# Neighbourhood attention layer on one core: output weights summed in memory by transfers, another order of the last products, bias tables laid out in memory, and a rearranged first step

## The chip, the cores and the metric

The kernel runs on one core of a Trainium2 chip. A core has TensorE (matrix products, PE in the profile; its weight loads are PEld), VectorE (DVE), ScalarE (ACT), GpSimd (POOL) and SyncE (SP), each with its own queue of instructions that it works through in order, and 16 DMA engines that serve transfers issued by SP, ACT and POOL. The metric is the device time of one execution in microseconds, the median of several runs. Less is better.

## The reference

One layer on 512 tokens (a grid of 8 rows by 64 columns), width 2048, 16 heads of 128, all float32:

```python
h = rms_norm(x, norm_pre)
q, k, v, z = split(h @ w_in, 4)            # w_in: 2048 x 8192
o = neighbourhood_attention(q, k, v, rpb)   # 8 x 16 window of tokens, bias rpb by relative place
y = (o * silu(z)) @ w_out                   # w_out: 2048 x 2048
out = x + rms_norm(y, norm_post)
```

The window covers all 8 rows and 16 columns, clipped at the edges of the grid. `rpb` holds 15 x 31 values for each head.

## The kernel before, in words

**Products.** Each product is taken from float32 operands split into two parts: `hi` (rounded, by a ScalarE copy, L241) and `lo` (the rest, by a VectorE subtraction, L242), and three of the four part products are summed: hi by hi, lo by hi, hi by lo. The left operand is the activations (tiles `a`, kept split in SBUF), the right one a 128 x 512 tile of weights that streams from memory.

**Steps.** Steps 0 to 7 compute the projection for two heads each. Step 8 and the last step, `LAST` = 9, compute the output product, the left and the right part of it. Steps 0 and 8 (`PLAIN`) are plain products of two halves, 32 slots of 12 matmuls. The other steps use a fast scheme on 2 x 2 blocks with seven products instead of eight: seven passes of 8 slots, 6 matmuls a slot. The passes have numbers 0 to 6 and accumulate in three chains X, Y, Z of two PSUM tiles each: passes 0 and 2 in X, 1, 3 and 5 in Y, 4 and 6 in Z. In the last step they run in the order `LATE`; before, that is 0, 1, 3, 4, 5, 6, 2.

**Weights of the seven passes.** Pass 0 uses block B11 in the tiles `T[0..7]`. Passes 1, 3 and 4 add B12, B22 and B21 to T in turn (L234, VectorE; the added block is a `raw` tile that a transfer has just brought); pass 4 then loads B12 into T; pass 5 uses B22 as it comes and adds it to T (L249), which pass 6 uses; pass 2 uses B21 as it comes. `raw` has four buffers.

**Order.** The slots are numbered through, m = 0 to 511. `prep(m)` splits the weights of slot m two slots ahead, and issues the loads of raws up to six slots ahead; the split weights have three buffers. `at(m, f)` puts f behind the matmuls of slot m: the attention of the heads of the pair before, all of whose work is spread over the slots of the next step (`HEAD`, `when`); the squares of x for the first norm (`square_x`, `begin`); evictions. A scheduler orders each engine's instructions by a plan of its own, except those issued through `sync`, `dve`, `act`, which keep the order of the program.

**The first step.** x, transposed, comes in 16 tiles (`load_x`), three slots ahead; each is scaled by the gain (L159) and split. Eight squares, each of 128 x 1024 of x in 0.5 MB, are loaded from slot 6 on and give the row sums; `rstd` turns them into `rc` at slot 28 (a power on POOL). The step's first half `U[0]` waits in PSUM and is evicted with the scale rc in slots 28 to 31 (`take_first`, L288), the second half in slot 31. Tiles of the pool `c` (six buffers of 128 x 1024) hold squares, evicted results and some x.

**Bias.** For each head one transfer on POOL brings overlapping rows of rpb (`braw`, L444), and three VectorE additions (L450) turn them with a mask into the table `bm` that the scores are added to. The gates are kept in memory and fetched again by transfers on POOL (L549, L559).

**The end.** Each of the four column quarters of the output needs a square sum over its rows (`finish`: a ScalarE square, a VectorE product with the gain); when the last quarter of a group of 128 rows is in, the row's factor `rcy` is computed (VectorE L666, POOL L667), and `final` adds the four quarters to the residual tiles `xres`, loaded before (`load_res`), and stores them. There are four such groups of rows: 2 and 3 are complete after pass 6, 0 and 1 after the two halves of the last pass, 2. The last pass does one half of its rows after the other, and so its eight weight tiles are all split beforehand, into tiles of `a` that are free by then.

Of the kernel before, what the change touches and what calls it, by code (L numbers as in the profile page):

```python
# [66 lines left out]
@with_exitstack  # L67
def na_block(ctx: ExitStack, tc: tile.TileContext, xT, x, gpre, gpost, w, rpb, mask, out):
    nc = tc.nc
    sync, dve, act = (InOrder(tc, e) for e in (nc.sync, nc.vector, nc.scalar))  # L70
    PSUM = bass.MemoryType.PSUM
# [155 lines left out]
    def prep(m):  # L227
        step, p, k = where(m)
        plain = step in PLAIN
        if step == 0 and p == 0:  # L230
            take_x(k)
        src = raws.pop(m) if is_raw(m) else T[k]
        if not plain and p in (1, 3, 4):
            nc.vector.tensor_tensor(T[k], T[k], src, ALU.add)  # L234
# [6 lines left out]
        nc.scalar.copy(hi, src)  # L241
# [41 lines left out]
    def take_first(n, j):  # L283
        c = C.setdefault(0, {})
        name = ("11", "12", "21", "22")[n + j // 2 * 2]
        if j % 2 == 0:
# [1 line left out]
        nc.scalar.activation(c[name][:, j % 2, :], U[n][j], AF.Copy, scale=rc[:, j : j + 1])  # L288

# [41 lines left out]
    def combine(step, p):  # L331
# [10 lines left out]
        elif p == 2:  # L342
            c["11"] = pair(f"c11_{step}")
            for s in range(2):
                nc.scalar.activation(c["11"][:, s, :], u[s], AF.Copy, scale=rc[:, s : s + 1])
        elif p == 3:
            c["22"] = pair(f"e_{step}")
            for s in range(2):
                nc.vector.tensor_tensor(c["22"][:, s, :], u[s], c["12"][:, s, :], ALU.subtract)
            nc.vector.tensor_tensor(c["21"], c["22"], c["21"], ALU.subtract)  # L350
        elif p == 4:
            for s in range(2):
                nc.vector.tensor_tensor(c["22"][:, s, :], u[s], c["22"][:, s, :], ALU.add)
        elif p == 5:
            for s in range(2):
                nc.vector.tensor_tensor(c["12"][:, s, :], u[s], c["12"][:, s, :], ALU.subtract)  # L356
            for s in range(2):
# [4 lines left out]
        elif step == LAST:
            c["11"] = pair(f"c11_{step}")
            for s in range(2):
                dve.tensor_tensor(c["21"][:, s, :], u[s], c["21"][:, s, :], ALU.subtract)
                dve.tensor_tensor(c["22"][:, s, :], c["22"][:, s, :], u[s], ALU.subtract)
                finish(2, 2 + s, c["21"][:, s, :])
                finish(3, 2 + s, c["22"][:, s, :])
# [72 lines left out]
    def load_bias(h):  # L441
        raw = sp.tile([P, L], F32, tag="braw", name=f"braw{h}")
        src = bass.AP(rpb.tensor, rpb.offset + h * 15 * TBL, [[1, 16], [TBL, 8], [1, 7 * TBL + 32]])
        nc.gpsimd.dma_start(raw[:, 0 : 7 * TBL + 32], src)  # L444
        bm_of[h] = (raw, sp.tile([P, 3, 256], F32, tag="bm", name=f"bm{h}"))

    def bias(h, i):
        raw, bm = bm_of[h]
        rev = bass.AP(raw.tensor, raw.offset + 7 * TBL + 31, [raw.ap[0], [-1, 32], [-TBL, 8]])
        nc.vector.tensor_tensor(  # L450
            bm[:, i, :].rearrange("p (a b) -> p a b", b=8),
            rev,
            mask_sb[:, i, :].unsqueeze(2).to_broadcast([P, 32, 8]),
            ALU.add,
        )

# [15 lines left out]
    def add_bias(h, a):  # L472
# [3 lines left out]
        for i in ((0, 1), (3, 2))[a]:  # L476
# [6 lines left out]
                in1=bm_of[h][1][:, (0, 1, 1, 2)[i], lo:hi],
# [169 lines left out]
    def finish(n, t, src, dst=None):  # L653
# [6 lines left out]
        nc.scalar.activation(rest, src, AF.Square, accum_out=part[:, t, i : i + 1])  # L660
        (dve if n > 1 else nc.vector).tensor_tensor(y, src, gb[n], ALU.mult)
        if i == 2:
            nc.vector.reduce_sum(ms3[:, col], part[:, t, 0:3], axis=mybir.AxisListType.X)
            nc.vector.tensor_scalar(ms3[:, col], ms3[:, col], 1.0 / D, EPS, ALU.mult, ALU.add)
        if i == 3:
            dve.tensor_scalar(msy[:, col], part[:, t, 3:4], 1.0 / D, ms3[:, col], ALU.mult, ALU.add)  # L666
            nc.gpsimd.tensor_tensor(rcy[:, col], msy[:, col], mhalf[:, 0:1], ALU.pow)  # L667
# [59 lines left out]

# [38 lines left out]
```

## Time and profile before

| | |
|---|---|
| median of 3 runs | 902.35 us (899.84 to 902.76) |
| profiled execution: its own time, its span | 903.68 us, 901.9 us |
| mean granted TensorE clock | 0.994 |
| busy share of the span | PE 98%, PEld 81%, DVE 84%, ACT 62%, POOL 3% |
| transfers | 163.32 MB, mean 181 GB/s |

How to read it: the span runs from the first to the last instruction. A busy share is an average over the whole span. Matmuls are pipelined, so that a busy PE can still be late; what a stretch lost is seen from the start times of its matmuls, compared with a stretch of the same work that nothing disturbs. In a row of the timeline the columns are start and length in us, engine, line, operation, output and inputs, and count; a bracket gives the idle time ahead of it and what ended it.

### The profile page before, as it was taken

The page shows a single profiled execution, that of the slowest core. Times are in us where ns is not written, and L with a number is a line of the kernel's source. Part 1 is how long each engine was busy: PE and PEld are TensorE (multiplying, and loading weights), DVE is VectorE, ACT ScalarE, POOL GpSimd, SP SyncE. Part 2 cuts the span into 40 slices and gives each one's busy share as a digit, 9 for nine tenths or more (in the row PEclk, how much of TensorE's full clock was granted, in tenths as well). Part 3 has the DMA queues.
Part 4 walks back from the last instruction along what each step waited for, and adds up shares of the span by engine and source line. Part 5 has one row for each costly group of instructions (what it writes and reads, how often), then busy time and mean ns, then how long its engine had stood idle before and what let it go on. Part 6 is the DMA issues. An engine that isn't in the chain of part 4 may idle for free. (4 is left out here: it accounts for less than half of the span.)

```text
span 901.9 us, 13169 instructions
## 1 busy us (share of the span) xinstructions
PE 880.9 (98%) x4184; PEld 731.3 (81%) x4184; DVE 755.3 (84%) x1415; ACT 561.2 (62%) x1089; POOL 29.7 (3%) x59
## 2 busy tenths in 40 slices
PE   9999999999999999999999999999999999999994
PEld 7878888888888888888888888888888788887773
DVE  5467879997989798989888987998799855887987
ACT  7566766575758575856585667566766755554461
POOL 1000000000000000000000000000010100000001
PEclk9999999999999999999999999999999999999998
DMA  8895357745773776377647764765587534549765
GB/s 256 237 258 131 105 138 210 217 130 162 219 214 111 190 227 192 95 218 210 176 112 219 210 176 110 239 200 149 137 278 205 157 93 119 158 122 254 245 179 186
DMA packets 85878, 163.32 MB, mean 181 GB/s; under 512 B 10017, under 2 KB 10017, under 8 KB 85809
## 3 DMA queue, kind: packets, MB, share of 16 engines
q1 hardware_dynamic: 82080, 151.56, 57.7%
q0 software_dynamic: 3296, 10.41, 4.2%
q8 instruction: 32, 0.52, 0.2%
q10 hardware_dynamic: 432, 0.53, 0.2%
q14 instruction: 38, 0.30, 0.1%
HBM read 154.59 MB, written 7.86 MB: 180 GB/s over the span
## 5 line engine op out<-in xcount | busy, mean ns | idle before, releaser
L241 ACT CAST hi<-t 128x512 fp32r<-128x512 f32 x320 | 196.8, 618 | 137.3 <-DVE lo L242 31.1
L242 DVE TENSOR_TENSOR lo<-t,hi 128x512 fp32r<-128x512 f32 x320 | 218.1, 687 | 25.8 <-ACT hi L241 24.9
L242 DVE TENSOR_TENSOR lo<-raw,hi 128x512 fp32r<-128x512 f32 x184 | 125.8, 689 | 62.8 <-ACT hi L241 50.3
L241 ACT CAST hi<-raw 128x512 fp32r<-128x512 f32 x184 | 113.6, 620 | 98.9 <-PE u L279 18.7
L234 DVE TENSOR_TENSOR t<-t,raw 128x512 f32<-128x512 f32 x192 | 128.5, 688 | 13.0 <-DMA raw<-in_w 12.5
L279 PE MATMUL u<-hi,a 128*128 128x512 f32 x512 | 133.1, 397 | 3.4 <-ACT hi L241 2.1
L279 PEld LDWEIGHTS u<-hi,a 128*128 128x128 f32 x512 | 96.2, 191 | 24.3 <-ACT hi L241 2.6
L279 PE MATMUL u<-lo,a 128*128 128x512 f32 x256 | 70.8, 390 | 0.0
L279 PEld LDWEIGHTS u<-lo,a 128*128 128x128 f32 x256 | 48.2, 188 | 10.1
L249 DVE TENSOR_TENSOR t<-t,raw 128x512 f32<-128x512 f32 x64 | 42.8, 688 | 1.2 <-DMA raw<-in_w 1.1
L149 DVE TENSOR_TENSOR a<-x,a 128x256 fp32r<-128x256 f32 (+1 forms) x24 | 11.6, 512 | 19.5 <-ACT a L148 19.5
L450 DVE TENSOR_TENSOR bm<-braw,mask_sb 128x256 f32<-128x256 f32 x48 | 27.4, 601 | 0.0
L322 PE MATMUL u1Y<-hi,a 128*128 128x512 f32 x96 | 26.8, 396 | 0.0
L322 PE MATMUL u6Y<-hi,a 128*128 128x512 f32 x96 | 26.8, 396 | 0.0
L322 PE MATMUL u5Y<-hi,a 128*128 128x512 f32 x96 | 26.8, 396 | 0.0
L322 PE MATMUL u7Y<-hi,a 128*128 128x512 f32 x96 | 26.8, 396 | 0.0
L322 PE MATMUL u3Y<-hi,a 128*128 128x512 f32 x96 | 26.8, 396 | 0.0
L322 PE MATMUL u4Y<-hi,a 128*128 128x512 f32 x96 | 26.8, 396 | 0.0
L322 PE MATMUL u2Y<-hi,a 128*128 128x512 f32 x96 | 26.8, 396 | 0.0
L322 PE MATMUL u9Y<-hi,a 128*128 128x512 f32 x96 | 26.6, 392 | 0.0
L444 POOL DMA_DIRECT2D braw<-in_rpb x16 | 8.5, 534 | 437.9 <-DVE bm L450 253.5
L322 PEld LDWEIGHTS u9Y<-hi,a 128*128 128x128 f32 x96 | 17.9, 188 | 4.3 <-ACT s L341 0.4
(444 smaller groups left out, 1953.2 us busy)
## 6 DMA issues: line engine op xcount, KB each, us to landing
raw<-in_w SPq DMA_DIRECT2D x384, 256.0 KB, 3.0
t<-in_w SPq DMA_DIRECT2D x128, 256.0 KB, 3.0
x<-in_xT SPq DMA_DIRECT2D x16, 256.0 KB, 4.4
xres<-in_x SPq DMA_DIRECT2D x16, 256.0 KB, 6.2
graw<-zm POOLq DMA_DIRECT2D x14, 256.0 KB, 3.7
out<-xres SPq DMA_DIRECT2D x14, 256.0 KB, 3.2
sq<-in_x SPq DMA_DIRECT2D x6, 512.0 KB, 9.4
braw<-in_rpb POOLq DMA_DIRECT2D x16, 184.0 KB, 3.6
```

Source lines behind the costliest of these rows:

```text
L149: (vector or nc.vector).tensor_tensor(lo, src, hi.bitcast(F32), ALU.subtract)
L234: nc.vector.tensor_tensor(T[k], T[k], src, ALU.add)
L241: nc.scalar.copy(hi, src)
L242: nc.vector.tensor_tensor(lo, src, hi.bitcast(F32), ALU.subtract)
L249: nc.vector.tensor_tensor(T[k], T[k], src, ALU.add)
L279: nc.tensor.matmul(U[n][j], l, r, start=k == 0 and i == 0, stop=k == KT - 1 and i == 2)
L322: nc.tensor.matmul(U[c][s], l, r, start=p in (0, 1, 4) and k == 0 and n == 0, stop=k == KH - 1 and n == 2, skip_group_check=True,)
L444: nc.gpsimd.dma_start(raw[:, 0 : 7 * TBL + 32], src)
L450: nc.vector.tensor_tensor(bm[:, i, :].rearrange("p (a b) -> p a b", b=8), rev, mask_sb[:, i, :].unsqueeze(2).to_broadcast([P, 32, 8]), ALU ...
```

## The change

- **Sums of W.** A new tile in memory, `wsum`, is filled with the four sums of blocks that the last step's passes 1, 3, 4 and 6 use: B11+B12, that +B22, that +B21, and B12+B22. For each of 8 tiles a sum is a copy from memory to memory and an accumulating transfer, 64 transfers in all, on POOL. They are issued from slot 32 on, 6 slots apart (later where the slot is in pass 2 or 5), each behind a one-column copy on ScalarE from a tile T in use and a one-column copy of that on POOL. The last step then loads each pass's tiles into T, a pass ahead, and makes no additions; only pass 2 still uses raws, which are loaded up to 24 slots ahead.
- **Order.** `LATE` becomes 0, 1, 3, 4, 6, 5, 2. The last pass's weights are split every second slot from the middle of the fifth pass on.
- **The end.** `finish` and `final` of row groups 2 and 3 are placed in the slots of the sixth pass (pass 5), and VectorE's instructions there no longer keep the program's order. Residual tiles are loaded at other slots, those of group 0 into T.
- **Bias.** The whole table of each head (128 x 3 x 256) is an input; a transfer on SP loads it. The three additions, the mask and the transfer on POOL go.
- **Gates** are stored and fetched on SP.
- **First step.** Squares are loaded from slot 10 on and squared 5 slots later; `rstd` is at slot 30. `U[0]` is evicted by plain copies in slots 17 to 20 and scaled in place in slot 31. x is fetched four slots ahead. The loads of T for step 1 keep the program's order.

The diff, cut:

```diff
-LATE = (0, 1, 3, 4, 5, 6, 2)
+LATE = (0, 1, 3, 4, 6, 5, 2)
...
     def load_t(step, q, k):
-        nc.sync.dma_start(T[k], w[step, q, k])
+        (sync if step == 1 and q == B11 else nc.sync).dma_start(T[k], w[step, q, k])
+    wsum = dp.tile([4, KH, P, L], F32, name="wsum")
+    LATE_W = {0: w[LAST, B11], 1: wsum[0], 3: wsum[1], 4: wsum[2], 5: w[LAST, B22], 6: wsum[3], 2: w[LAST, B21]}
+    SUMS = ((0, w[LAST, B11], B12), (1, wsum[0], B22), (2, wsum[1], B21), (3, w[LAST, B12], B22))
+    turns = cp.tile([P, 2, 64], F32, name="turns")
+    def sum_w(j, t):
+        i, add, k = j // 16, j // 8 % 2, j % 8
+        nc.scalar.copy(turns[:, 0, j : j + 1], t[:, 0:1])
+        pool.tensor_copy(turns[:, 1, j : j + 1], turns[:, 0, j : j + 1])
+        o, src, q = SUMS[i]
+        if add:
+            pool.dma_start(wsum[o, k], w[LAST, q, k], accum_op=ALU.add, max_dma_last_dim=8192)
+        else:
+            pool.dma_start(wsum[o, k], src[k], max_dma_last_dim=8192)
...
-        return step in PLAIN or p not in (0, 6)
+        return step in PLAIN or (p == 2 if step == LAST else p not in (0, 6))
...
-        e = max(m - 6 if m < N - KH else 0, seq[i - NRAW] if i >= NRAW else 0)
+        e = max(m - (6 if m < N - KH else 24), seq[i - NRAW] if i >= NRAW else 0)
...
-        if not plain and p in (1, 3, 4):
+        if step < NSTEP and not plain and p in (1, 3, 4):
             nc.vector.tensor_tensor(T[k], T[k], src, ALU.add)
...
-        if plain:
+        if step == LAST:
+            i = LATE.index(p)
+            if i + 2 < NPASS:
+                nc.sync.dma_start(T[k], LATE_W[LATE[i + 1]][k])
+        elif plain:
...
-        nc.scalar.activation(c[name][:, j % 2, :], U[n][j], AF.Copy, scale=rc[:, j : j + 1])
+        if n == 0:
+            nc.scalar.copy(c[name][:, j % 2, :], U[n][j])
+        else:
+            nc.scalar.activation(c[name][:, j % 2, :], U[n][j], AF.Copy, scale=rc[:, j : j + 1])
...
     def load_bias(h):
-        raw = sp.tile([P, L], F32, tag="braw", name=f"braw{h}")
...
-        nc.gpsimd.dma_start(raw[:, 0 : 7 * TBL + 32], src)
...
+        bm_of[h] = sp.tile([P, 3, 256], F32, tag="bm", name=f"bm{h}")
+        nc.sync.dma_start(bm_of[h], rpb[h])
...
-            nc.gpsimd.dma_start(graw[h], z_of[h])
+            nc.sync.dma_start(graw[h], z_of[h])
...
-        nc.gpsimd.dma_start(X[h], graw[h])
+        nc.sync.dma_start(X[h], graw[h])
...
-        for i in range(3):
-            at(when(h, i) if late else when(h, 0) - 7 + i, bias, h, i)
...
-        at(6 + 2 * i, begin, i)
-        at(12 + 2 * i, lambda i=i: pending.pop(i)())
-    at(8, lambda: nc.gpsimd.dma_start(mask_sb, mask))
-    at(28, rstd)
+        at(10 + 2 * i, begin, i)
+        at(15 + 2 * i, lambda i=i: pending.pop(i)())
+    at(30, rstd)
     for j in range(4):
-        at(28 + j, take_first, 0, j)
+        at(KT + 1 + j, take_first, 0, j)
+        at(FIRST - 1, lambda j=j: scale_c(C[0][("11", "21")[j // 2]], j % 2, j // 2 * 2))
...
-    for k in range(KH):
-        t, q = divmod(k, 4)
-        at(base(LAST) + KH + k, load_res, 2 + t, q)
-        at(base(LAST) + (5 * KH + 2 * q + 1 if t == 0 else 2 * KH + 2 * q), load_res, t, q)
+    for i, (t, q) in enumerate((t, q) for t in (2, 3, 1) for q in range(4)):
+        at(base(LAST) + (KH + 7 * i // 2 if i < KH else 4 * KH + 4 + 2 * q), load_res, t, q)
+    for q in range(4):
+        at(base(LAST) + 5 * KH + q, load_res, 0, q)
+    for j in range(64):
+        m = base(1) + 6 * j
+        while where(m)[1] in (2, 5):
+            m += 1
+        at(m, sum_w, j, T[where(m)[2]])
     for s in range(2):
-        at(base(LAST) + 6 * KH + 1 + s, final, 2 + s)
+        for n, key in ((2, "21"), (3, "22")):
+            at(base(LAST) + 5 * KH + 1 + 2 * s, lambda n=n, key=key, s=s: finish(n, 2 + s, C[LAST][key][:, s, :]))
+        for q in range(4):
+            at(base(LAST) + 5 * KH + 5 + 2 * s + q // 2, final, 2 + s, (q,))
...
-        if N - 2 * KH <= m + AHEAD < N - KH:
-            prep(m + AHEAD + KH)
-        if 0 <= m and m + 3 < KT:
-            load_x(m + 3)
+        if m >= N - 3 * KH + 4 and m % 2 == 0 and m < N - KH + 4:
+            prep(N - KH + (m - (N - 3 * KH + 4)) // 2)
+        if 0 <= m and m + 4 < KT:
+            load_x(m + 4)
```

In `combine`, `finish` and `final`, `dve.` becomes `nc.vector.`.

More of the change, by code (lines that the diff above doesn't have):

```diff
@@ L67, in na_block @@
 @with_exitstack
-def na_block(ctx: ExitStack, tc: tile.TileContext, xT, x, gpre, gpost, w, rpb, mask, out):
+def na_block(ctx: ExitStack, tc: tile.TileContext, xT, x, gpre, gpost, w, rpb, out):
     nc = tc.nc
-    sync, dve, act = (InOrder(tc, e) for e in (nc.sync, nc.vector, nc.scalar))
+    sync, dve, act, pool = (InOrder(tc, e) for e in (nc.sync, nc.vector, nc.scalar, nc.gpsimd))
     PSUM = bass.MemoryType.PSUM
@@ L99, in na_block @@
     nc.gpsimd.memset(mhalf, -0.5)
-    mask_sb = cp.tile([P, 3, 32], F32, name="mask_sb")
     edge = {}
@@ L364, in combine @@
             for s in range(2):
[L365 to L368, printed above, removed]
+                nc.vector.tensor_tensor(c["21"][:, s, :], u[s], c["21"][:, s, :], ALU.subtract)
+                nc.vector.tensor_tensor(c["22"][:, s, :], c["22"][:, s, :], u[s], ALU.subtract)
         else:
@@ L441, in load_bias @@
     def load_bias(h):
-        raw = sp.tile([P, L], F32, tag="braw", name=f"braw{h}")
[L443 to L455, printed above, removed]
+        bm_of[h] = sp.tile([P, 3, 256], F32, tag="bm", name=f"bm{h}")
+        nc.sync.dma_start(bm_of[h], rpb[h])
     WIN = {0: (0, 64), 1: (64, 256), 2: (192, 0), 3: (256, 192)}
@@ L482, in add_bias @@
                 in0=s_of[h, a][:, base + lo : base + hi],
[L483 removed]
+                in1=bm_of[h][:, (0, 1, 1, 2)[i], lo:hi],
                 op0=ALU.add,
@@ L625, in na_block @@
     for i in range(8):
-        at(6 + 2 * i, begin, i)
-        at(12 + 2 * i, lambda i=i: pending.pop(i)())
-    at(8, lambda: nc.gpsimd.dma_start(mask_sb, mask))
-    at(28, rstd)
+        at(10 + 2 * i, begin, i)
+        at(15 + 2 * i, lambda i=i: pending.pop(i)())
+    at(30, rstd)
     for j in range(4):
-        at(28 + j, take_first, 0, j)
+        at(KT + 1 + j, take_first, 0, j)
+        at(FIRST - 1, lambda j=j: scale_c(C[0][("11", "21")[j // 2]], j % 2, j // 2 * 2))
+    for j in range(4):
         at(FIRST - 1, take_first, 1, j)
@@ L660, in finish @@
         nc.scalar.activation(rest, src, AF.Square, accum_out=part[:, t, i : i + 1])
-        (dve if n > 1 else nc.vector).tensor_tensor(y, src, gb[n], ALU.mult)
+        nc.vector.tensor_tensor(y, src, gb[n], ALU.mult)
         if i == 2:
@@ L665, in finish, with final @@
         if i == 3:
-            dve.tensor_scalar(msy[:, col], part[:, t, 3:4], 1.0 / D, ms3[:, col], ALU.mult, ALU.add)
+            nc.vector.tensor_scalar(msy[:, col], part[:, t, 3:4], 1.0 / D, ms3[:, col], ALU.mult, ALU.add)
             nc.gpsimd.tensor_tensor(rcy[:, col], msy[:, col], mhalf[:, 0:1], ALU.pow)
-    def final(t):
+    def final(t, qs=range(4)):
         col = slice(t, t + 1)
-        for q in range(4):
+        for q in qs:
             r = xres[t, q]
-            dve.scalar_tensor_tensor(r, yg[q, t], rcy[:, col], r, ALU.mult, ALU.add)
+            nc.vector.scalar_tensor_tensor(r, yg[q, t], rcy[:, col], r, ALU.mult, ALU.add)
             eng = nc.scalar if t == 1 and q % 2 else nc.sync
@@ L683, in load_res @@
         else:
-            if q % 2 == 0:
-                xres["c", q] = ag.tile([P, 2, L], F32, tag=f"a{q // 2}_1", name=f"xres{t}{q}")
-            xres[t, q] = xres["c", q - q % 2][:, q % 2, :]
+            xres[t, q] = T[q]
         sync.dma_start(xres[t, q], x_v[16 * t : 16 * t + 16, :, q * L : (q + 1) * L])
@@ L690, in na_block @@
         at(base(NSTEP) + 11 + n, load_gb, n)
-    for k in range(KH):
-        t, q = divmod(k, 4)
-        at(base(LAST) + KH + k, load_res, 2 + t, q)
-        at(base(LAST) + (5 * KH + 2 * q + 1 if t == 0 else 2 * KH + 2 * q), load_res, t, q)
-    for s in range(2):
-        at(base(LAST) + 6 * KH + 1 + s, final, 2 + s)
-    for k in range(3):
+    for i, (t, q) in enumerate((t, q) for t in (2, 3, 1) for q in range(4)):
[7 more added lines that the diff above has]
+        at(m, sum_w, j, T[where(m)[2]])
+    for s in range(2):
+        for n, key in ((2, "21"), (3, "22")):
+            at(base(LAST) + 5 * KH + 1 + 2 * s, lambda n=n, key=key, s=s: finish(n, 2 + s, C[LAST][key][:, s, :]))
+        for q in range(4):
+            at(base(LAST) + 5 * KH + 5 + 2 * s + q // 2, final, 2 + s, (q,))
+    for k in range(4):
         load_x(k)
-        load_raw(k)
+        if k < 3:
+            load_raw(k)
     for m in range(-AHEAD, N):
@@ L713, in na_block, with _bias @@
             f()
-def _mask():
-    m = np.full((P, 3, GRID_W // 2), NEG, np.float32)
+def _bias(rpb):
+    flat = np.pad(rpb[:, ::-1, ::-1], ((0, 0), (0, 0), (8, TBL - 39))).reshape(HEADS, -1)
+    c, r, a, b = np.ogrid[0:16, 0:ROWS, 0:32, 0:ROWS]
+    rel = flat[:, c + TBL * r + 7 * TBL + 31 - a - TBL * b].reshape(HEADS, P, 256)
+    tab = np.full((HEADS, P, 3, 256), NEG, np.float32)
     for typ, i in ((0, 0), (1, 1), (2, 3)):
@@ L754 @@
         "w": w,
-        "rpb": rpb,
-        "mask": _mask(),
+        "rpb": _bias(np.asarray(na_rpb)[0]),
     }
@@ L762 @@
     with tile.TileContext(nc) as tc:
-        na_block(tc, *(aps[k] for k in ("xT", "x", "gpre", "gpost", "w", "rpb", "mask")), out)
+        na_block(tc, *(aps[k] for k in ("xT", "x", "gpre", "gpost", "w", "rpb")), out)
     r = run_bass_kernel_spmd(nc, [{f"in_{k}": v for k, v in feeds.items()}], core_ids=[0])
```

6 lines of the change are left out of this document (3 added, 3 removed).

## The prediction

> **What bounds the kernel now.** I read the page's shares first, then TensorE's own timeline pass by pass, then the windows around each place where that timeline is late, and last the chain behind the last matmul. The page:
>
> ```profile
> span 901.9 us, 13169 instructions
> PE 880.9 (98%) x4184; PEld 731.3 (81%) x4184; DVE 755.3 (84%) x1415; ACT 561.2 (62%) x1089; POOL 29.7 (3%) x59
> ...
> q1 hardware_dynamic: 82080, 151.56, 57.7%
> ...
> raw<-in_w SPq DMA_DIRECT2D x384, 256.0 KB, 3.0
> ```
>
> TensorE is the bound, and the change does not alter its matmuls. So only TensorE's late places and the ends can give time back. The windows (columns: length, busy time of PE, PEld, DVE, ACT, POOL with counts, granted clock, DMA share, GB/s) name them:
>
> ```profile
> 45.00:52.00 7.00, 4.87 (x15) 3.58 (x14) 2.84 (x5) 5.41 (x10) 0.00 (x0) 0.76 0.84 229
> ...
> 98.00:807.00 709.00, 707.75 (x3443) 590.78 (x3442) 618.32 (x1168) 458.65 (x899) 22.79 (x42) 1.00 0.59 174
> ...
> 818.00:845.00 27.00, 24.24 (x100) 17.94 (x100) 19.53 (x32) 11.99 (x21) 0.00 (x0) 1.00 0.97 258
> ```
>
> The long middle (steps 1 to 8, 709 us) idles 1.25 us in all: nothing is to be had there, only lost. The last step by the first matmul of each pass (and the last matmul of all), from TensorE's timeline:
>
> ```profile
> 807.18 1.07 PE L322 MATMUL u9X<-hi,a 128*128 128x512 f32 x4
> ...
> 818.06 1.07 PE L322 MATMUL u9Y<-hi,a 128*128 128x512 f32 x4
> ...
> 844.49 1.07 PE L322 MATMUL u9Z<-hi,a 128*128 128x512 f32 x4
> ...
> 855.37 1.07 PE L322 MATMUL u9Y<-hi,a 128*128 128x512 f32 x4
> ...
> 866.25 1.07 PE L322 MATMUL u9Z<-hi,a 128*128 128x512 f32 x4
> ...
> 878.29 0.61 PE L322 MATMUL u9X<-a,a 128*128 128x512 f32 x2
> ...
> 888.95 0.39 PE L322 MATMUL u9X<-a 128*128 128x512 f32 x1
> ```
>
> An undisturbed pass of 8 slots takes 818.06 - 807.18 = 10.88 us, 1.36 a slot. Passes 1 and 3 together take 26.43 instead of 21.76: **4.7 us lost**. Pass 6 takes 12.04: **1.2 lost**. The last matmul ends at 889.34, so 12.6 us of the span lie behind it. The first step, where an undisturbed slot of 12 matmuls takes 15.54 - 12.81 = 2.73:
>
> ```profile
> 6.19 2.38 PE L279 MATMUL u<-hi,a 128*128 128x512 f32 x8
> ...
> 12.81 1.98 PE L279 MATMUL u<-hi,a 128*128 128x512 f32 x8
> ...
> 15.54 1.98 PE L279 MATMUL u<-hi,a 128*128 128x512 f32 x8
> ...
> 40.26 0.43 SPq L140 DMA_DIRECT2D x<-in_xT  x1
> 40.74 0.56 SPq L64 DMA_DIRECT2D sq<-in_x  x1
> ...
> 42.73 1.98 PE L279 MATMUL u<-hi,a 128*128 128x512 f32 x8
> ...
> 46.47 0.72 ACT L159 ACTIVATE x<-x,gcol 128x512 f32<-128x512 f32 x1 [1.94 <-DMA x<-in_xT]
> ...
> 47.75 3.69 PE L279 MATMUL u<-hi,a 128*128 128x512 f32 x8 [2.13 <-ACT hi L241]
> ...
> 52.20 0.63 PE L279 MATMUL u<-hi,a 128*128 128x512 f32 x2
> ```
>
> The first two slots take 6.62 for 5.46: **1.2 lost**. Slots 14 and 15 (42.73 is slot 13) end at 52.20 after 9.47 for two slots counted from 42.73 and 5.46 due: **4.0 lost**, of which 2.1 is idle and the rest a lowered clock (0.76 in the window above; the eight matmuls take 3.69 instead of 1.98). The cause stands in the rows: ScalarE, in order, waits 1.94 for the last x tile, which was issued 6 us before among transfers of squares.
>
> **The change, part by part.**
>
> *First step, -5.2.* Squares begin at slots 10, 12, ... instead of 6, 8, ...; x tiles are fetched 4 slots ahead instead of 3, so the last is issued at slot 11 with one square ahead of it instead of three; the early loads of T are now in program order. Until slot 10 only x and the weights are fetched, 2 x 0.262 MB per 2.73 us = 192 GB/s, under the 229 that the window at 45 carried. So the 4.0 go. The 1.2 at the start goes with the first bias and the mask, which shared the first transfers (they leave the POOL queue); -1.0 of it is taken. Bounds: 0 and -5.2. Against it stands the squares' new place: eight of 0.52 MB from slot 10, two in flight at a time, because the two tiles of plain copies (slots 17 to 20) now hold two of the six buffers. SyncE then waits about a slot for a square's buffer, and the weight loads behind it with it; four raw buffers cover four slots, 10.9 us. Cost 0, to +4.0 if the cover is short (the stall that is there now).
>
> *Towards step 1, +0.3.* The four scaled evictions become plain copies earlier, and four scalings in place are added at the step's end, beside the other four scaled evictions. What is behind them:
>
> ```profile
> L379 ACT ACTIVATE s<-s,rc 128x512 f32<-128x512 f32 x28 | 19.4, 717 | 0.0
> ...
> 98.53 1.26 ACT L288 ACTIVATE c<-u,rc 128x512 f32<-128x512 f32 x2
> ...
> 103.90 0.60 PE L403 MATMUL tk<-ident,c 128*128 128x128 f32 x4
> ```
>
> 4 x 0.717 = 2.9 us more on ScalarE, against 103.90 - 99.79 = 4.1 us until TensorE transposes the result. Hidden, with 1.2 left; +0.3 is taken, range 0 to +2.
>
> *Bias.* 48 VectorE additions go and 16 loads of 0.39 MB replace 16 of 0.18 MB, on SP instead of POOL; 14 stores and 14 fetches of gates move to SP too.
>
> ```profile
> L450 DVE TENSOR_TENSOR bm<-braw,mask_sb 128x256 f32<-128x256 f32 x48 | 27.4, 601 | 0.0
> ...
> L444 POOL DMA_DIRECT2D braw<-in_rpb x16 | 8.5, 534 | 437.9 <-DVE bm L450 253.5
> ```
>
> 29 us of VectorE work vanish where VectorE hides behind TensorE: 0. SP gets 44 more issues of about 0.5 us and three kinds of wait: for the last use of the bias tile, for the gate, for T. Each is emitted slots after what it waits for (4 slots for the bias, 2 for the gate), while weights run 4 to 6 slots ahead. Cost 0, bounded by a raw's cover, +1.
>
> *The sums of W by transfer, 64 of 0.262 MB, 0 to steps 1 to 7 (+0.5 taken).* Queue q1 needs 0.577 x 901.9 / 151.56 = 3.43 us of all 16 engines per MB, so a plain copy costs 0.90. An accumulating one has no row; it is at least 0.90, and at twice that 1.8. Sum 32 x (0.90 + 1.8) = 86 us over 709: the share rises from 0.59 to 0.71, with the bias to 0.73. The transfers are spaced 6 slots (8 us), each behind a one-column copy on ScalarE and one on POOL. ScalarE gains 64 such copies; at the 0.19 us of the nearest one-column row that is 12 us beside 250 idle ones:
>
> ```profile
> L499 ACT ACTIVATION_READ_ACCUMULATOR p<-p,nm 128x1 f32 x32 | 6.0, 188 | 0.0
> ```
>
> A copy placed in the pass where T has just been reloaded waits for that load (3 us) and holds ScalarE up to a slot; three slots of split weights cover it. POOL does nothing else by then. What the sums can cost is the delay of a raw: it lands after 3.0, its buffer comes round after 4 x 1.36 = 5.4, and the split weights stand three slots ahead, so about 3.7 more are free. Range 0 to +4.
>
> [...]
>
> *Last step's loads, -4.4.* Now passes 1 and 3 wait for additions that wait for raws:
>
> ```profile
> raw<-in_w SPq DMA_DIRECT2D x17, 256.0 KB, 5.6
> xres<-in_x SPq DMA_DIRECT2D x12, 256.0 KB, 7.3
> ...
> DVE t L234 <- DMA raw<-in_w: 7.7, 9, 1.6
> ```
>
> (807 to 840 us; raws land after 5.6, over the 5.4 of their ring.) The additions go, T is loaded a whole pass ahead (10.9 us), and the residual tiles come every 3.5 slots instead of every slot. But the bytes do not shrink: in slots 8 to 32, 24 T, 8 residual and 4 raw tiles, 9.4 MB in 32.6 us = 289 GB/s, against 258 at share 0.97. That is some 3 us behind by slot 32, with 10.9 - 5.6 = 5.3 to spare. So -4.4; bounds 0 and -4.7.
>
> *Order 6 before 5, +0.3 and -0.3.* Passes 4 and 6 use the same PSUM tiles and now follow each other: TensorE waits for two VectorE additions (0.6 each) out of them. The same happens today between passes 1 and 3 behind a ScalarE copy, inside the 4.7. The halves finish 0.68 apart, so one addition is mostly covered: +0.3 (0 to +1.3). The 1.2 of pass 6 came from double preparation beside 0.6 us additions; preparation is now every second slot, but pass 5 inherits four subtractions and four multiplications: -0.3 (-1.2 to +1).
>
> *Tail, -1.8.* VectorE's timeline:
>
> ```profile
> 884.00 1.41 DVE L64 SCALAR_TENSOR_TENSOR xres<-y,rcy,xres 128x512 f32<-128x512 f32 x2
> ...
> 889.90 0.20 DVE L64 TENSOR_SCALAR msy<-part,ms 128x1 f32<-128x1 f32 x1
> 890.76 1.41 DVE L64 SCALAR_TENSOR_TENSOR xres<-y,rcy,xres 128x512 f32<-128x512 f32 x2 [0.65 <-POOL rcy L667]
> ...
> 894.01 0.20 DVE L64 TENSOR_SCALAR msy<-part,ms 128x1 f32<-128x1 f32 x1
> ...
> 896.87 0.75 DVE L64 SCALAR_TENSOR_TENSOR xres<-s,rcy,xres 128x512 f32<-128x512 f32 x1
> ```
>
> The last half's row sum (894.01) stands 4.7 behind the last matmul, queued behind the residual additions of the three other groups of rows. Eight of them (groups 2 and 3; 0.67 each, 5.3 us) can now run a pass earlier. But that pass is full: 8 subtractions and multiplications, 10 splits and 8 residual additions are 18 x 0.6 + 5.3 = 16 us in 10.9, so about 5 us spill into the last pass. Its own work is 7 operations of 0.6, 0.6 of small ones and four residual additions, 7.5 of 10.9; so some 2 us hang over the last matmul, then 0.6 + 0.75 + 2.7 for the last half: the end at +6.1 instead of +8.3 (897.62). With no spill it is +4.6. I take -1.8; bounds -3.7 and +1.
>
> **Sum.** -5.0 (first step: -1.0 - 4.0) + 0.3 + 0.5 - 4.4 + 0.3 - 0.3 - 1.8 = -10.4. The profiled execution took 903.68 us for its span of 901.9, so 893.3; it stands 1.3 above the median of 902.35, so the median after is **892**.
>
> **Rivals.** (a) *Slower: the sums hold up the raws.* If a summing transfer delays a raw by d, TensorE loses d - 3.7 each time; about 45 of the 64 fall in passes that use raws. From d = 3.94 the whole gain of 10.4 is gone; at 4.1 it is 45 x 0.4 = 18, so 910. For it: raws that land after 5.6, barely over their ring, already go with a loss of 4.7 in the last step. Against: the share in the middle is 0.59, and a plain copy costs 0.90. 0.12.
> (b) *The last step stays bound by its transfers*, 289 asked and 258 given: the 4.4 stay, 896.5. For: share 0.97 today; against: ten us of lead. 0.13.
> (c) *The squares stall again*, later: a wait of two us with its slow clock, 896. For: two buffers instead of four; against: the bytes are spread and x is in by then. 0.12.
> (d) *Everything goes*: no spill in the tail (-3.7), pass 6 without loss (-1.2), no small costs: 888. 0.13.
> (e) *The change's gains are undone by small waits* (ScalarE behind reloaded T, SP behind gates), about 10 us: 902, no change. 0.06.
> (f) *The clock dips though the wait goes*: then only the idle 2.1 of the 4.0 comes back, 894. For: nothing in the rows but that the dip outlasts the idle. Against: the dip follows the only long idle, and the clock is 1.00 in every other window shown. 0.04. [...]
>
> The forecast itself, 889.5 to 895: 0.40.
>
> **Numbers.** Forecast 892. From (d) with its lower bound to the worse mixes of (b), (c) and (e): 886 to 900. Faster by over 0.3% (2.7 us, about what the runs of 899.84 to 902.76 can tell apart): 0.40 + 0.13 + 0.12 + 0.13 + 0.04 = 0.82; within 0.3%: 0.06; slower: 0.12.
>
> **What would show it.** No idle of TensorE near slot 14 and a clock of 1.00 in the first 100 us; passes of the last step 10.9 us apart; no addition L234 there; DMA share of the middle near 0.72 with TensorE's idle there still near 1 us; last residual addition about 6 us behind the last matmul. Wrong it would be by raws landing after 7 us in the middle, by a wait of TensorE for T in the last step, or by the residual additions still queued ahead of the last row sum.

## The result, and the profile after

The change made the kernel slower: 930.38 us (929.56 to 932.54) against 901.44 (899.84 to 902.76) on the same chip, ratio 1.0326 (95% interval 1.0299 to 1.0352). 892 was forecast, with a range of 886 to 900. The page of after (shares, transfer queues, issues with their size and median us to landing):

```profile
span 927.8 us, 13231 instructions
PE 887.4 (96%) x4184; PEld 731.9 (79%) x4184; DVE 714.1 (77%) x1335; ACT 564.1 (61%) x1157; POOL 68.6 (7%) x142
...
q0 software_dynamic: 3072, 16.78, 8.3%
...
raw<-in_w SPq DMA_DIRECT2D x352, 256.0 KB, 2.9
...
wsum<-in_w POOLq DMA_DIRECT2D x48, 256.0 KB, 4.8
```

TensorE does the same work and is busy for less of the span. The share of q0, the queue of the new transfers, is modest, and the median raw lands after 2.9 us (3.0 before): neither row betrays 26 us more. The windows do (columns as in the prediction: first half's end, the middle, passes 1 and 3, the seam of passes 4 and 6):

```profile
45.00:52.00 7.00, 7.00 (x33) 5.79 (x32) 3.71 (x8) 3.16 (x6) 0.00 (x0) 1.00 0.67 183
...
93.00:839.00 746.00, 718.04 (x3440) 591.76 (x3439) 597.17 (x1123) 462.06 (x963) 61.09 (x124) 0.99 0.63 191
...
850.00:872.00 22.00, 22.00 (x97) 17.89 (x96) 10.99 (x17) 13.66 (x24) 0.00 (x0) 1.00 0.82 251
...
883.00:896.00 13.00, 11.78 (x53) 9.45 (x52) 9.38 (x16) 6.48 (x12) 0.00 (x0) 1.00 0.93 286
```

In the middle TensorE now idles 746.0 - 718.0 = 28 us, where it idled 1.25. Its busy time there also grew, from 707.75 to 718.04 us for the same matmuls, at a granted clock of 0.99 instead of 1.00. TensorE's timeline gives the ledger:

```profile
93.12 1.07 PE L347 MATMUL u1X<-hi,a 128*128 128x512 f32 x4
...
839.51 1.07 PE L347 MATMUL u9X<-hi,a 128*128 128x512 f32 x4
...
850.39 1.07 PE L347 MATMUL u9Y<-hi,a 128*128 128x512 f32 x4
...
872.49 1.07 PE L347 MATMUL u9Z<-hi,a 128*128 128x512 f32 x4
...
885.20 0.70 PE L347 MATMUL u9Z<-hi,a 128*128 128x512 f32 x2 [1.22 <-DVE e L378]
...
896.18 1.07 PE L347 MATMUL u9Y<-hi,a 128*128 128x512 f32 x4
...
917.26 0.39 PE L347 MATMUL u9X<-a 128*128 128x512 f32 x1
```

Step 1 started at 98.45 before:

```profile
98.45 1.07 PE L322 MATMUL u1X<-hi,a 128*128 128x512 f32 x4
```

| stretch, us | before | after | moved | forecast |
|---|---|---|---|---|
| to step 1's first matmul | 98.45 | 93.12 | -5.3 | -4.7 |
| steps 1 to 8 | 708.7 | 746.4 | **+37.7** | +0.5 (0 to +4) |
| last step's matmuls | 82.2 | 78.1 | -4.0 | -4.4 |
| behind the last matmul | 12.6 | 10.1 | -2.4 | -1.8 |
| span | 901.9 | 927.8 | +25.9 | -10.4 |

Three of four terms are right within 0.6; the middle is wrong by 37. What TensorE's suppliers wait for, from the list of waits of the whole span, nearly all of it in the middle (total us, times, longest):

```profile
ACT turns L136 <- DMA t<-in_w: 55.2, 25, 6.0
...
ACT hi L258 <- DMA raw<-in_w: 25.7, 19, 3.9
DVE t L251 <- DMA raw<-in_w: 22.5, 20, 3.9
...
ACT turns L136 <- DVE t L251: 12.0, 8, 2.7
```

Before, the casts (`hi`) waited 10.4 us for raws (8 times) and the additions (`t`) 12.5 (19 times) in the whole span, of which only 2.8 and 4.8 in the middle. The largest of these waits is new: the one-column copy `turns`, which only spaces the transfers, holds ScalarE for 55 us. One such place in the timeline of all engines:

```profile
362.31 0.76 POOL L64 DMA_DIRECT2D wsum<-in_w  x1
...
363.24 0.75 POOL L64 DMA_DIRECT2D wsum<-in_w  x1
...
367.22 0.61 PE L347 MATMUL u4X<-lo,a 128*128 128x512 f32 x2
...
369.99 0.19 ACT L136 COPY turns<-t 128x1 f32<-128x1 f32 x1 [6.03 <-DMA t<-in_w]
370.09 1.13 ACT L258 CAST hi<-t 128x512 fp32r<-128x512 f32 x2
...
370.76 1.93 PE L347 MATMUL u4X<-hi,a 128*128 128x512 f32 x4 [2.92 <-ACT hi L258]
```

The copy reads a tile T whose reload has not landed. ScalarE, in order, stands 6.03 us in front of it; the casts (L258) that make split weights stand behind; TensorE runs out and idles 2.92, and its next four matmuls take 1.93 instead of 1.07. In a second kind of place ScalarE's copies wait under a microsecond and it is a raw that is late:

```profile
217.94 0.75 POOL L64 DMA_DIRECT2D wsum<-in_w  x1
...
218.56 1.04 POOL L64 DMA_DIRECT2D wsum<-in_w  x1
...
222.75 0.75 POOL L64 DMA_DIRECT2D wsum<-in_w  x1
...
226.65 0.69 DVE L251 TENSOR_TENSOR t<-t,raw 128x512 f32<-128x512 f32 x1 [3.88 <-DMA raw<-in_w]
```

Behind three such transfers the two raws issued from 222 on land after 7.4 us, against the median of 2.9. VectorE, in order, stands 3.88 us in front of its addition, the subtractions (`lo`) behind it come late, and TensorE then idles 2.60:

```profile
raw<-in_w SPq DMA_DIRECT2D x2, 256.0 KB, 7.4
```

```profile
230.53 0.85 PE L347 MATMUL u2Y<-lo,a 128*128 128x512 f32 x2 [2.60 <-DVE lo L259]
```

### The profile page after: what moved, and what is told of

Read it like the earlier page. It is cut to its first block, busy times and chain, and to the rows that moved or that the text cites. A ratio compares the mean times of both kernels' runs of the same rounds, so it can differ in the third digit from the quotient of the medians.

```text
span 927.8 us, 13231 instructions
## 1 busy us (share of the span) xinstructions
PE 887.4 (96%) x4184; PEld 731.9 (79%) x4184; DVE 714.1 (77%) x1335; ACT 564.1 (61%) x1157; POOL 68.6 (7%) x142
## 3 DMA queue, kind: packets, MB, share of 16 engines
q0 software_dynamic: 3072, 16.78, 8.3%
HBM read 174.60 MB, written 24.64 MB: 215 GB/s over the span
## 4 chain that ended last, share of the span: by engine, by line
PE 67%; DMA 15%; DVE 10%; ACT 4%; issue 3%; SPq 0%; POOL 0%; DVEq 0%; POOLq 0%; ACTq 0%
PE u L300 17%; DMA raw<-in_w 10%; DMA t<-in_w 5%; DVE lo L259 4%; PE u9Y L347 4%; PE u2Y L347 3%; PE u7Y L347 3%; PE u4Y L347 3%; PE u3Y L347 3%; PE u5Y L347 3%; PE s L478 3%; PE u4Z L347 2%; ACT hi L258 2%; PE u7X L347 2%; PE u9Z L347 2%
## 5 line engine op out<-in xcount | busy, mean ns | idle before, releaser
L259 DVE TENSOR_TENSOR lo<-t,hi 128x512 fp32r<-128x512 f32 x328 | 221.6, 685 | 66.3 <-ACT hi L258 63.3
L258 ACT CAST hi<-t 128x512 fp32r<-128x512 f32 x328 | 199.2, 617 | 89.5 <-DVE lo L259 17.7
L259 DVE TENSOR_TENSOR lo<-raw,hi 128x512 fp32r<-128x512 f32 x176 | 120.5, 688 | 71.3 <-ACT hi L258 49.8
L258 ACT CAST hi<-raw 128x512 fp32r<-128x512 f32 x176 | 108.8, 621 | 97.4 <-DMA raw<-in_w 25.7
L300 PE MATMUL u<-hi,a 128*128 128x512 f32 x512 | 130.8, 391 | 1.3 <-DVE e L395 1.3
L251 DVE TENSOR_TENSOR t<-t,raw 128x512 f32<-128x512 f32 x168 | 112.0, 685 | 22.9 <-DMA raw<-in_w 22.5
L64 POOL COPY turns<-turns 128x1 f32<-128x1 f32 x64 | 26.9, 420 | 579.4 <-ACT turns L136 579.4
L136 ACT COPY turns<-t 128x1 f32<-128x1 f32 x64 | 11.1, 190 | 71.6 <-DMA t<-in_w 55.2
L270 DVE TENSOR_TENSOR t<-t,raw 128x512 f32<-128x512 f32 x56 | 37.3, 683 | 8.8 <-DMA raw<-in_w 8.8
L64 POOL DMA_DIRECT2D wsum<-in_w x48 | 33.2, 699 | 0.6
L347 PE MATMUL u4X<-hi,a 128*128 128x512 f32 x64 | 19.4, 422 | 2.9 <-ACT hi L258 2.9
```

What stands on the lines that cost most here:

```text
L64: return lambda *args, **kwargs: self.tc.keep_in_program_order(f(*args, **kwargs))
L136: nc.scalar.copy(turns[:, 0, j : j + 1], t[:, 0:1])
L300: nc.tensor.matmul(U[n][j], l, r, start=k == 0 and i == 0, stop=k == KT - 1 and i == 2)
L347: nc.tensor.matmul(U[c][s], l, r, start=p in (0, 1, 4) and k == 0 and n == 0, stop=k == KH - 1 and n == 2, skip_group_check=True,)
```

## The experiments

Two causes stand against each other: (A) ScalarE held by the copy that reads T, (B) the transfers, which delay the loads of raws. A third, (C), is SP's new loads, stores and waits. All runs are timed beside the kernel before on the same chip (its median: 899.05 for the first four, 901.22 for the next four, then 900.35 and 900.54), so a difference between times of two tables can be off by about 2 us. e2, e3, e5 and e12 leave sums out and do not compute the reference's product; they serve the timing only. The profiles were read for the length of the middle as in the ledger.

**First four: the copy, the transfers, both.**

```diff
 e1_copy_reads_hi: the copy reads split weights that are there already
-        at(m, sum_w, j, T[where(m)[2]])
+        at(m, lambda j=j, m=m: sum_w(j, W[m + AHEAD][0].bitcast(F32)))
```

> The kernel after, with one thing changed: ScalarE's one-column copy ahead of each summing transfer reads the hi tile that ScalarE has itself just written, instead of a tile T that may be on its way from memory. The 64 transfers, their slots and both copies stay. Steps 1 to 8 took 746.4 us after and 708.7 before (first matmul of step 1 to first matmul of the last step), 37.7 more. Theory A (ScalarE, in order, is held by the copy while T is loaded: 55.2 us in 25 waits): the 37.7 go nearly whole, 893 to 897 us. Theory B (the transfers delay the raws): little changes, about 925. Theory C (SP's new loads, stores and waits delay the raws): about 925.

```diff
 e2_no_transfers: the copies stay, the 64 transfers go
-            pool.dma_start(wsum[o, k], ...)                       # both forms
-    LATE_W = {0: w[LAST, B11], 1: wsum[0], 3: wsum[1], 4: wsum[2], ..., 6: wsum[3], ...}
+    LATE_W = {0: w[LAST, B11], 1: w[LAST, B12], 3: w[LAST, B22], 4: w[LAST, B21], ..., 6: w[LAST, B12], ...}
```

> The kernel after without the 64 summing transfers; both one-column copies stay, reading T. The last step loads the plain blocks of W in the place of their sums, so its products are not those of the reference. Theory A (ScalarE held by the copies): still about 922 to 930 us. Theory B (transfers): 891 to 897. Theory C (SP): about 925.

```diff
 e3_no_sums: as e2, and the copies go too
-    for j in range(64):
-        ...
-        at(m, sum_w, j, T[where(m)[2]])
```

> The kernel after without transfers and without the copies ahead of them; the last step loads plain blocks of W, so its products are not those of the reference. Theories A and B: 889 to 893 us, the sum that the prediction made without its term for the sums (891.5). Theory C (SP's new loads, stores and waits): still about 925.

```diff
 e4_hi_no_bunching: as e1, every 6 slots exactly
-        while where(m)[1] in (2, 5):
-            m += 1
```

> As the run whose copy reads hi, and in addition the transfers stand exactly 6 slots apart, where the kernel after moves those of passes 2 and 5 to the next pass, so that two or three come at once. In the kernel after three came within 5 us at 218 to 223, landed after 6.3 to 7.8 us, and a raw beside them took 7.4. Theory A: as the run whose copy reads hi, within 1 us. Theory B: faster than that run by several us, since bunched transfers delay a raw most.

| | time, us | ratio to before (95%) | middle |
|---|---|---|---|
| after | 930.38 | 1.0326 (1.0299 to 1.0352) | 746.4 |
| e1 copy reads hi | 909.88 | 1.0102 (1.0071 to 1.0132) | 728.9 |
| e2 no transfers | 896.52 | 0.9959 (0.9940 to 0.9978) | 714.8 |
| e3 no sums | 893.25 | 0.9917 (0.9886 to 0.9948) | 712.0 |
| e4 hi, no bunching | 907.98 | 1.0077 (1.0046 to 1.0108) | 725.0 |

Both causes are real, and together they cost more than their sum. The hold costs 930.4 - 909.9 = 20.5 us beside the transfers and 896.5 - 893.3 = 3.3 without them; the transfers cost 909.9 - 893.3 = 16.6 without the hold and 33.9 with it. So neither theory alone holds, and (C) is not the main cause: e3 keeps SP's new issues. The waits of e2:

```profile
ACT turns L134 <- DMA t<-in_w: 38.8, 21, 4.1
```

38.8 us of waiting, but the longest is 4.1, about what three slots of split weights last (3 x 1.36); the 6.0 beside the transfers is longer. Where TensorE then idled shows the two paths apart. These are its waits in the middle, summed by what ended them: the split weights (`hi`, `lo`), or VectorE's splits of k and q for the attention (rows `tz <- k..l` and `s <- q..l`):

| TensorE's waits in the middle, us | for split weights | for splits of k and q |
|---|---|---|
| after | 14.7 | 11.3 |
| e1 copy reads hi | 1.6 | 11.4 |
| e2 no transfers | 3.3 | 0.9 |
| e3 no sums | 0.3 | 1.6 |

The hold makes the split weights late. The transfers alone (e1) hardly do; they reach TensorE by another way, always at the same place, the second head's k in each of steps 1 to 7. One such place in e1:

```profile
496.14 0.69 DVE L251 TENSOR_TENSOR t<-t,raw 128x512 f32<-128x512 f32 x1 [1.31 <-DMA raw<-in_w]
...
498.07 0.69 DVE L439 TENSOR_TENSOR k9l<-tk,k9h 128x512 fp32r<-128x512 f32 x1
...
498.81 0.44 PE L426 MATMUL tz<-ident,s 128*128 128x128 f32 x2 [3.01 <-DVE k9l L439]
```

VectorE's additions wait for raws, its split of k (`k9l`) stands behind them, and the transpose `tz`, which needs the PSUM tile that this split reads (two tiles in turn), holds TensorE for 3.01 us. Of the 64 transfers 12 fall into slot 24 of a step, two slots ahead of the second head; nine of these were moved there out of pass 2 by the rule that spares passes 2 and 5. Evening out these bunches (e4) takes the waits for k and q down to 8.6 us but is worth only 1.9 in time (909.23 to 910.85 against 906.49 to 908.64), less than the several us expected by theory B. e3 has the rest of the change and no sums: its gain, 0.83% (0.5 to 1.1), is what the change brings with the work of the sums left out altogether.

**What in a transfer costs.** Adding, length of pieces, or occupancy at the wrong time; against it, quieter slots and a longer ring of raws. All with e1's copy.

```diff
 e5_adds_as_copies
-            pool.dma_start(wsum[o, k], w[LAST, q, k], accum_op=ALU.add, max_dma_last_dim=8192)
+            pool.dma_start(wsum[o, k], w[LAST, q, k], max_dma_last_dim=8192)
 e7_pieces_2k: 2048 for 8192 in both forms
 e8_quiet_slots: nine a step, at its slots 0, 2, ... 16 (passes 0, 1 and the start of 2)
-        m = base(1) + 6 * j
-        while where(m)[1] in (2, 5):
-            m += 1
+        m = base(1 + j // 9) + 2 * (j % 9)
 e9_five_raws
-NRAW = 4
+NRAW = 5
```

> As the run whose copy reads hi (909.9 us), with the 32 accumulating transfers turned into plain copies of the same size, so wsum holds single blocks and not sums. With no transfers and no wait of ScalarE the kernel took about 893, so 64 transfers cost some 16. If it is the adding (a second read, a slower path) that holds up the raws: 897 to 902 us, since only half of the transfers added. If it is any transfer of 0.26 MB beside the raws: 906 to 910.

> As the run whose copy reads hi (909.9 us), with the transfers cut into pieces of a quarter of the length (2048 instead of 8192). If a raw is held up behind long pieces in the 16 engines (the raws' own pieces are 2 KB): 897 to 903 us. If it is the engines' time as such: 908 to 915, shorter pieces making no better use of it.

> As the run whose copy reads hi (909.9 us), with the 64 transfers in the first 18 slots of each of steps 1 to 7, every second slot, where the DMA engines were busy 0.2 to 0.5 of the time in the kernel before, and none later in the step, where they were busy 0.6 to 0.9. If the transfers cost only where they meet the dense loads of raws: 893 to 898 us. If they cost wherever they are: 905 to 912, as the total is the same.

> As the run whose copy reads hi (909.9 us), with five raw buffers instead of four, so that a raw has 6.8 us from issue to use instead of 5.4. If the loss comes through the ring of raws (a raw that lands 1 to 4 us late): 899 to 905 us. If it comes through T's loads or another way: 908 to 911.

| | time, us | ratio (95%) | middle |
|---|---|---|---|
| e5 adds as copies | 901.50 | 1.0007 (0.9991 to 1.0023) | |
| e7 pieces of 2048 | 911.44 | 1.0105 (1.0083 to 1.0128) | |
| e8 quiet slots | 898.97 | 0.9968 (0.9951 to 0.9986) | 713.6 |
| e9 five raws | 897.85 | 0.9953 (0.9932 to 0.9974) | 716.8 |

What an addition takes stands in the queue's share, first e1, then e5:

```profile
span 909.1 us, 13241 instructions
...
q0 software_dynamic: 3072, 16.78, 9.0%
```

```profile
span 899.0 us, 13241 instructions
...
q0 software_dynamic: 3072, 16.78, 5.9%
```

64 copies took 0.059 x 899.0 = 53.0 us of all 16 engines, 0.83 each (0.90 was estimated). 32 copies and 32 additions took 81.8, so an addition 1.73, 2.1 copies. In the kernel after, at 8.3%, the same sum gives 1.58 an addition. Why an addition takes longer isn't shown: the pages of e1 and e5 give the same 174.60 MB read and 24.64 MB written. Turning additions to copies gives back 909.9 - 901.5 = 8.4, half of the transfers' 16.6; the rest is paid for plain copies too. The length of pieces does nothing that shows (queue q0 has 7168 packets in e7, 3072 in e1). A fifth raw gives 12.0 and quieter slots 10.9, with as many transfers: the windows of the middle show that they remove idle time, not occupancy (e1, then e9, then e8, whose profiled execution took 895.54, 3.4 below its median):

```profile
93.00:822.00 729.00, 713.83 (x3442) 592.25 (x3442) 598.54 (x1123) 465.81 (x964) 62.68 (x128) 1.00 0.67 196
```

```profile
93.00:810.00 717.00, 710.23 (x3443) 589.58 (x3442) 597.80 (x1123) 467.55 (x966) 81.98 (x128) 1.00 0.68 200
```

```profile
93.00:806.00 713.00, 708.60 (x3439) 589.77 (x3438) 596.10 (x1121) 462.49 (x963) 57.42 (x128) 1.00 0.69 201
```

Shares of 0.67 to 0.69, and idle times of 15.2, 6.8 and 4.4 us: the mean load is not what costs. TensorE's waits for the splits of k and q fall from 11.4 to 4.5 (e9) and 2.6 us (e8).

**Do the cures add, and what of SP's new issues?**

```diff
 w1_quiet_five: e8 and NRAW = 5
 w2_quiet_five_pool: w1, with bias and gates issued on POOL again
-        nc.sync.dma_start(bm_of[h], rpb[h])
+        nc.gpsimd.dma_start(bm_of[h], rpb[h])
   ... the same for graw[h] and X[h]
 e12_no_sums_pool: e3 with the same three on POOL
 e11_after_five: after with NRAW = 5 alone
```

> Three cures at once: the copy reads hi, the transfers stand in the quiet slots, five raw buffers. Each of the last two alone took some 11 to 12 us off 909.9. If both act on the same waits for raws, they do not add: 893 to 897 us, the floor being the kernel without sums, 893.3. If they act on different places, the same floor is met more closely, 892 to 894. Slower than 898 would mean that the quiet slots have a cost of their own.

> As the run with all three cures, with the loads of the bias and the stores and loads of the gates on POOL again, as before the change. Theory C (on SP these wait at the head of the queue, 24 us for the bias tile in the kernel after, and hold back raws): 2 to 4 us faster. If their waits are covered: the same within 1 us.

> The kernel without sums (893.3 us, plain blocks of W in the last step, so not the reference's products), with bias and gates on POOL again. Its steps 1 to 8 still take 712.0 us where the kernel before took 708.7. Theory C (SP's queue): those 3 us go, about 890. Otherwise 893.

> The kernel after with five raw buffers and nothing else; ScalarE's copies still read T. If ScalarE's hold is a loss of its own (T's load, delayed by the transfers, stands in ScalarE's way whatever the raws do): 912 to 920 us, 15 to 20 above the run with five raws whose copy reads hi (897.9). If the hold only hurts because raws are late at the same time: 898 to 904.

| | time, us | ratio (95%) |
|---|---|---|
| w1 | 897.52 | 0.9977 (0.9962 to 0.9991) |
| w2 | 899.45 | 0.9992 (0.9972 to 1.0013) |
| e12 | 891.08 | 0.9904 (0.9874 to 0.9933) |
| e11 | 910.72 | 1.0121 (1.0093 to 1.0148) |

The cures don't add: w1 is no better than e9 or e8 alone, and all three cut the same waits (3.1 us for the splits of k and q in w1). Moving bias and gates off SP shows nothing beside the sums (w1 and w2 overlap) and 2.2 us without them, in which the intervals of e12 and e3 overlap too: that SP's issues cost anything isn't shown. e11 gives the hold once more: 910.72 - 897.85 = 12.9 us with five raws, so the fifth raw does not cure a held ScalarE. Its waits:

```profile
ACT turns L136 <- DMA t<-in_w: 38.8, 23, 4.2
...
ACT turns L136 <- DVE t L251: 19.0, 7, 3.8
```

The same 38.8 us for T as in e2, and nearly the same longest wait (4.2 against 4.1), but e2 loses 3.3 and e11 12.9. So the length of the longest wait doesn't explain the loss by itself. In e11 TensorE waits 5.8 us for split weights and 8.5 for splits of k and q, in e9 0.7 and 4.5; the copy's wait behind VectorE's late additions, 19.0, is the candidate and wasn't tried.

**Is any sum needed?** The last step's gain was put down to loads of T in place of additions and to spread residual tiles. v1 starts from the kernel before and keeps its additions and order of passes; it takes the first step, the bias tables (issued on POOL), a fifth raw, and the change's places for residual tiles: the eight of groups 2 and 3 are 3.5 slots apart, and the four of group 1 come 20 slots later, out of passes 1 and 3.

```diff
 v1_no_sums_added, against the kernel before
-NRAW = 4
+NRAW = 5
...
-        at(base(LAST) + KH + k, load_res, 2 + t, q)
-        at(base(LAST) + (5 * KH + 2 * q + 1 if t == 0 else 2 * KH + 2 * q), load_res, t, q)
+        at(base(LAST) + KH + 7 * k // 2, load_res, 2 + t, q)
+        at(base(LAST) + (5 * KH + 2 * q + 1 if t == 0 else 4 * KH + 4 + 2 * q), load_res, t, q)
 v2_residuals_bunched: v1 with the two old lines of load_res
 v3_four_raws: v1 with NRAW = 4
```

> The kernel before with the first step of the change, its bias tables (loaded on POOL), five raw buffers, and the residual tiles of the last step spaced as in the change; the additions of W stay on VectorE and the order of the passes stays. Theory P (only sums made ahead cure the last step): passes 1 and 3 there still take some 26 us, 895 to 897. Theory Q (the last step's loss was a ring of raws that was too short beside bunched residual tiles): passes 1 and 3 take 22, the whole 890 to 893, below every kernel with sums in memory.

> The same with the residual tiles where the kernel before has them, one a slot. Theory Q: if five raws are enough by themselves, as with the spacing; if the bunching is the cause, 3 to 4 us more.

> The spaced version with four raws, as before. Theory Q: if the spacing is enough by itself, as with five raws; if the ring is the cause, 3 to 4 us more.

| | time, us | ratio (95%) | middle | passes 1 and 3 |
|---|---|---|---|---|
| v1 | **891.78** | 0.9905 (0.9883 to 0.9928) | 706.8 | 22.05 |
| v2 | 896.86 | 0.9955 (0.9939 to 0.9971) | | 26.08 |
| v3 | 893.96 | 0.9931 (0.9904 to 0.9959) | 709.1 | 22.06 |

TensorE's timeline, first matmuls of passes 1 and 4, v1, then v2:

```profile
810.67 1.07 PE L324 MATMUL u9Y<-hi,a 128*128 128x512 f32 x4
...
832.72 1.07 PE L324 MATMUL u9Z<-hi,a 128*128 128x512 f32 x4
```

```profile
811.06 1.07 PE L324 MATMUL u9Y<-hi,a 128*128 128x512 f32 x4
...
837.14 1.08 PE L324 MATMUL u9Z<-hi,a 128*128 128x512 f32 x4
```

Moving these residual loads is worth 4.0 us there and 5.1 in all (896.86 - 891.78). Median landings between 800 and 840 us, v1, then v2, and what the additions (L233) of v2 then waited for in passes 1 and 3:

```profile
raw<-in_w SPq DMA_DIRECT2D x22, 256.0 KB, 3.7
xres<-in_x SPq DMA_DIRECT2D x7, 256.0 KB, 4.4
```

```profile
raw<-in_w SPq DMA_DIRECT2D x22, 256.0 KB, 5.8
xres<-in_x SPq DMA_DIRECT2D x12, 256.0 KB, 7.7
```

```profile
DVE t L233 <- DMA raw<-in_w: 6.6, 11, 1.3
```

A ring of five raws lasts 6.8 us, so v2's median of 5.8 is inside it, and yet its additions waited 11 times: again the late raws count, not the median. In v1 no addition waits for a raw in passes 1 and 3, and TensorE does not idle there. v1 beats both kernels; v3, with four raws, is about 2 us behind it (893.42 to 894.91 against 891.38 to 892.08; the middle is 2.3 longer).

## Why the prediction was wrong, by its own steps

- *First step, -5.0 and +0.3:* right; it measured -5.3. The window at 45 has no idle and a clock of 1.00, so the dip went with the wait, and rival (f) is gone. The squares did not stall it again (c): from 6 to 93 us TensorE has no idle. (The two slots that the prediction counted from 42.73 are 13 and 14.)
- *The sums of W, +0.5, range 0 to +4:* **the step that failed; it measured +37.7 with what else moved in the middle** (+3.3 in e3, which has no sums). The occupancy was sized rightly: 1.73 and 0.83 us a transfer (1.8 and 0.90 were forecast), share 0.63 (0.67 in e1, whose span is shorter; 0.73 was forecast). The factor of two behind the 1.8 was the author's estimate, and before has no accumulating transfer that shows it; e1 and e5 give 2.1. Two sentences behind it were wrong. The first, that about 3.7 us more are free, took the median landing of a raw (3.0) and the lead of the split weights for the whole cover. Late raws land after 7.4, the prediction's own sign of being wrong (over 7), against the 5.4 after which the buffer comes round; and the cover is the split weights' alone. In e1 TensorE lost 1.6 us there, so for them it nearly held. The 11.4 us went by a path that the prediction did not count: VectorE, in order, waits for raws with its additions, and TensorE needs VectorE's split of k soon after. Rival (a) had the cause and the place, the middle. That its 910 is e1's 909.9 is luck: it has TensorE lose 0.4 us at some 45 transfers (37 fall in passes that use raws), where e1 shows 7 waits of up to 3.0 for k. Its chance of 0.12 was too low, since the "against" was the mean share. The other sentence, that a copy behind T "holds ScalarE up to a slot; three slots of split weights cover it", took the reload of T at 3 us. ScalarE's wait is up to 6.0 with the transfers beside it, and the hold comes on top of late raws: 20.5 us in the runs that tell it apart, 12.9 with five raws. Rival (e) named the hold only among small waits, though the same kind of wait (1.94 of ScalarE for an x tile) was the stall that the first step's gain was counted from.
- *SP's 44 more issues, 0:* open. e3, without sums, has a middle of 712.0 against v3's 709.1 with bias and gates on POOL; e12 is 2.2 faster than e3 and has a middle of 709.6 in its profile, the same direction, but the times' intervals overlap.
- *Last step's loads, -4.4:* right in size (22.10 for passes 1 and 3 against 26.43: -4.3), but the cause was not told apart. The prediction credits loads of T, additions that go and the spread of residual tiles together; the last is enough. The additions waited for raws because the residual tiles came one a slot; v3 gets the same 22.06 with additions, four raws and no sums. Rival (b), 289 asked against 258 given, is also gone: the window moved 251 at a share of 0.82, without idle.
- *Order 6 before 5, +0.3 and -0.3:* sum right, the parts too small. Passes 4 and 6 take 896.18 - 872.49 = 23.69 for 21.76, 1.9 more. Of this 1.22 is idle in front of pass 6's first matmuls, as the additions (L378) start late in VectorE's queue, and some 0.6 are two matmuls of the last pass that now run in between. In exchange, passes 5 and 2 take 917.65 - 896.18 = 21.47. The four passes together took 44.85 before and 45.16 after.
- *Tail, -1.8:* right, -2.4, in part by luck. The last row sum starts 1.9 us behind the last matmul (4.7 before; 2 forecast) and the last residual addition ends at +5.5 (6.1 forecast). The spill into the last pass is there too, but it is over by 913.4: VectorE then idles 1.49 for ScalarE's square of the first half. What stands ahead of the last row sum is the four residual additions of that half, not the spill.

```profile
914.85 0.69 DVE L671 TENSOR_TENSOR c<-u9X,gpost 128x512 f32<-128x512 f32 x1 [1.49 <-ACT ysq L670]
...
919.57 0.20 DVE L676 TENSOR_SCALAR msy<-part,ms 128x1 f32<-128x1 f32 x1
...
922.43 0.74 DVE L683 SCALAR_TENSOR_TENSOR xres<-s,rcy,xres 128x512 f32<-128x512 f32 x1
```

Open: why w1 and e9, with nothing held and five raws, stay 4 us above e3 (TensorE's waits for the splits of k and q, 3.1 and 4.5 us against 1.6, are a part of it), and how much of e3's middle (+3.3 over before) is SP.

## What to carry to other kernels

Background transfers must be priced against the latest loads they meet (raws that landed after 7.4 us here), not against the mean share or the median landing (0.63 and 2.9 us here); make the ring of buffers deeper or choose the slots before adding bytes (12.0 and 10.9 us here). And price a late load on every engine that waits for it: a lead of three slots covered the split weights in e1 but for 1.6 us, not the other results of the same in-order VectorE (11.4 us). An instruction that only paces something must read data that is surely there: here a copy waited up to 6.03 us for the load of a tile, and the casts behind it on ScalarE, in order, waited too. And before replacing work that "waits for loads", spread the loads that collide with it; here moved residual loads gave the last step's 4 us by themselves, without the 64 transfers.

## What the hardware showed that was not expected

An accumulating transfer from memory to memory took 1.73 us of all 16 engines per 256 KB in e1, 2.1 times a copy's 0.83 in e5. A `max_dma_last_dim` of 2048 instead of 8192 left the kernel's time where it was (911.4 against 909.9). The clock fell again after an idle of 2.92 us (four matmuls in 1.93 instead of 1.07, granted clock 0.56 from 370.7 to 373.0). The length of the idle alone doesn't decide it here: the clock falls after idles of 2.13 (before, 0.62 from 47.7 to 52.2) and 2.60 (after, 0.61 from 230.5 to 232.8), and behind one of 2.79 (after) it is still 1.00 (512.2 to 516.0).
